# A decoder layer on one core: branch b's values projected 512 columns wide, gates and a merge projection as filler, q's factor moved into the sigmoid

## The chip, the cores and the metric

The kernel runs on one core of a Trainium2 chip. The time is that of the device, in microseconds, from the first to the last instruction with what little lies around it. The engines are TensorE (PE), VectorE (DVE), ScalarE (ACT), GpSimd (POOL) and SyncE (SP), which issues nearly all DMAs. Each works through its own list of instructions in order, and waits at an instruction until what it needs is there.

## The reference, cut to what matters

One layer for 512 tokens of width 1024, in float32:

```python
h = rms_norm(x, g_mix)
qa, ka, va, qb, kb, vb, gates = jnp.split(h @ w_in, IN_SPLITS, axis=-1)
ya = moba_attention(rope(qa), rope(ka), va)             # 8 heads of 64, causal softmax
yb = stick_breaking_attention(qb, kb, vb)               # 8 heads of 64
#   z = q k^T / 8;  a = sigmoid(z) * (product of 1 - sigmoid(z) over the later keys)
g = sigmoid(gates + b_gate)                             # 2 x 1024
x = x + (g[0] * (ya @ w_branch_a) + g[1] * (yb @ w_branch_b)) @ w_out
u_gate, u_val = split(causal_depthwise_conv(rms_norm(x, g_ffn) @ w_up))
x = x + (silu(u_gate) * u_val) @ w_down                 # 2816 wide
return rms_norm(x, g_final)
```

With 512 tokens and blocks of 256, branch a's attention (moba) is a causal softmax over all keys.

## The kernel before

**Products.** Every large float32 product is made of three matmuls of rounded parts: both operands are split into a high part (`hi`, an ACT copy to a shorter format) and the rest (`lo`, a DVE subtraction), and hi.hi, hi.lo and lo.hi are added up in PSUM (`mm3`, called a triple here). `wload` fetches 512 KB of weights by DMA into `raw`, ACT makes `whi` (L67), DVE makes `wlo` (L68); there are three buffers of each, so a split waits until TensorE is through with the weights three loads back.

**Order.** TensorE's instructions run in the order in which the code is written (`manual_schedule`); those of DVE, ACT, POOL and SP are ordered by a scheduler when the kernel is built.

**The stages.** First `qk0`, the projection of branch a's first q and k from `xg` (8 tiles of x times g_mix, split, not yet normalised), while DVE adds up the squares `ssq`; a product of `ssq` with ones gives the row sums, `rstd_cols` and `rsqrt` (L114 to L131) turn them into r1, a 128x4 tile, and `bcast_rows` transposes r1 into `rb`, a tile with r along the columns. It scales everything that was projected from `xg`. Then `vproj_a` projects branch a's values, 512 columns a matmul. Then the attention: `attend(branch, pairs, gaps)` works on four heads (two pairs) at a time, twice for each branch. Its steps are `score` for a unit of query tiles (unit 0 has tiles 0 and 1, unit 1 tile 2, unit 2 tile 3), the weights on DVE, ACT and (branch b) POOL, and `turn`, the transposes of the weights of a unit and pair into the PSUM tile `tp`, of which there is one; ACT (branch b, and odd units of a) or DVE copies it to `aT`. Branch a's weights are maxima (L327), exponentials with their sums, and a multiply (L337); branch b's are two sigmoids, selects for the diagonal on POOL, scans (L357) and a multiply (L359). After the last step the attention products `av` follow, and ACT and DVE split their result into `ya` or `yb`.

**Filler.** Between two steps `fill(gap)` puts so many triples of other work into TensorE's list: the rest of branch a's q and k (`moba_qk`, whose results are rotated on DVE), branch b's q and k (`sb_qk`), branch b's values (`vproj_b`, 256 columns a matmul, half a unit each), and the first gates. Each such projection accumulates into one of two PSUM banks (`mm`), so the next but one can't start before DVE or ACT have taken its result out. What is left of the fillers runs after the last attention product (`fill(1000)`). The merge then makes, for each of 8 column tiles, the projections of `ya` and of `yb`, each multiplied by its gate. Behind it come W_out, the feed-forward part and the final norm, which the change leaves alone.

## Time and profile before

| | |
|---|---|
| median of 3 runs | 746.32 us (746.0 to 746.59) |
| the profiled execution | 746.52 us, of which 744.8 us are the span from first to last instruction |
| granted TensorE clock, mean | 0.998 |
| busy, share of the span | PE 99%, DVE 60%, ACT 41%, POOL 3% |
| matmuls on PE | 3890 |

The profile shows one execution: its page gives busy shares, waits and the chain of work that ended last, and its trace can be asked for a timeline of any stretch. In the rows a matmul's `us` is its length, and lengths overlap: what counts for the time is the distance from start to start. `x4` behind a row means four instructions in one row. Buffer numbers are left out.

### The profile page before, as it was taken

Reading aid. Unit: us, or ns where it says so; the run is one execution under the profiler, and the core shown is the slowest. Engines: PE = TensorE matmul, PEld = TensorE weight load, DVE = VectorE, ACT = ScalarE, POOL = GpSimd, SP = SyncE. Lnnn points to the kernel's source line nnn. Section 1 sums busy time; section 2 is a strip of 40 time slices with the busy share of each in tenths; the row PEclk is TensorE's granted clock in tenths of the full one; section 3 lists DMA queues with packets and bytes.
Section 4 is the critical chain, followed back from the end, with each engine's and each line's share of the span. In section 5 each row is a group of like instructions: output and inputs, shape, how many; then the busy total and the mean of one; then the engine's idle time right before and its main releaser. Section 6 shows DMA issues by size and latency. Waiting matters only on the chain.

```text
span 744.8 us, 9628 instructions
## 1 busy us (share of the span) xinstructions
PE 734.5 (99%) x3890; PEld 610.5 (82%) x3890; DVE 449.2 (60%) x635; ACT 306.5 (41%) x437; POOL 21.7 (3%) x40
## 2 busy tenths in 40 slices
PE   9999999999999999999999999999999999999996
PEld 6788888879788888888888888888888888888885
DVE  6868876692964544545658767777676774121233
ACT  6345453563652332324335444443544442121233
POOL 0000000320310000000000000000000000000000
PEclk9999999999999999999999999999999999999999
DMA  8332211121225323223232232323223232323203
GB/s 311 118 96 75 75 41 57 41 78 53 87 85 173 111 84 114 85 94 105 90 108 86 90 108 85 114 85 103 95 89 110 85 113 88 111 86 113 85 29 113
DMA packets 22364, 72.03 MB, mean 97 GB/s; under 512 B 2480, under 2 KB 3120, under 8 KB 22320
## 3 DMA queue, kind: packets, MB, share of 16 engines
q1 hardware_dynamic: 21600, 70.24, 28.4%
q10 hardware_dynamic: 720, 1.18, 0.4%
q8 instruction: 30, 0.49, 0.3%
q14 instruction: 14, 0.11, 0.1%
HBM read 69.31 MB, written 2.10 MB: 96 GB/s over the span
## 4 chain that ended last, share of the span: by engine, by line
PE 79%; issue 19%; DVE 1%; ACT 0%; POOL 0%; POOLq 0%; DVEq 0%; ACTq 0%
PE mm L72 20%; PE mm L74 20%; PE mm L73 20%; PE d L74 5%; PE d L73 5%; PE d L72 5%; PE tp L404 1%; PE tp L386 1%; PE sc L319 1%; DVE R L357 1%; PE d L553 0%; DVE a L359 0%; DVE wlo L68 0%; PE tp L117 0%; DVE on L592 0%
## 5 line engine op out<-in xcount | busy, mean ns | idle before, releaser
L67 ACT ACTIVATE whi<-raw 128x1024 fp32r<-128x1024 f32 (+2 forms) x128 | 130.1, 1021 | 225.5 <-PE mm L73 76.3
L68 DVE TENSOR_TENSOR wlo<-raw,whi 128x1024 fp32r<-128x1024 f32 (+2 forms) x128 | 149.6, 1174 | 88.8 <-ACT whi L67 87.7
L72 PE MATMUL mm<-h,whi 128*128 128x512 f32 x352 | 137.1, 390 | 0.0
L74 PE MATMUL mm<-h,wlo 128*128 128x512 f32 x352 | 137.0, 389 | 0.0
L73 PE MATMUL mm<-h,whi 128*128 128x512 f32 x352 | 136.9, 389 | 0.0
L72 PE MATMUL mm<-xg,whi 128*128 128x512 f32 x224 | 89.9, 401 | 0.0
L74 PE MATMUL mm<-xg,wlo 128*128 128x512 f32 x224 | 87.4, 390 | 0.0
L73 PE MATMUL mm<-xg,whi 128*128 128x512 f32 x224 | 87.3, 390 | 0.0
L73 PEld LDWEIGHTS mm<-h,whi 128*128 128x128 f32 x352 | 66.1, 188 | 13.8
L72 PEld LDWEIGHTS mm<-h,whi 128*128 128x128 f32 x352 | 66.1, 188 | 13.7
L74 PEld LDWEIGHTS mm<-h,wlo 128*128 128x128 f32 x352 | 66.1, 188 | 13.6
L72 PE MATMUL d<-whi,gT 128*128 128x512 f32 x176 | 69.2, 393 | 0.0
L73 PE MATMUL d<-wlo,gT 128*128 128x512 f32 x176 | 68.5, 389 | 0.0
L74 PE MATMUL d<-whi,gT 128*128 128x512 f32 x176 | 68.5, 389 | 0.0
L526 DVE TENSOR_TENSOR u<-mm,rb 128x512 f32<-128x512 f32 x44 | 30.2, 688 | 38.3 <-PE mm L74 38.3
L72 PEld LDWEIGHTS mm<-xg,whi 128*128 128x128 f32 x224 | 42.1, 188 | 9.7 <-issue 1.4
L74 PEld LDWEIGHTS mm<-xg,wlo 128*128 128x128 f32 x224 | 42.1, 188 | 9.1
L73 PEld LDWEIGHTS mm<-xg,whi 128*128 128x128 f32 x224 | 42.2, 188 | 7.8
L74 PEld LDWEIGHTS d<-whi,gT 128*128 128x128 f32 x176 | 33.0, 188 | 6.8
L73 PEld LDWEIGHTS d<-wlo,gT 128*128 128x128 f32 x176 | 33.1, 188 | 6.6
L72 PEld LDWEIGHTS d<-whi,gT 128*128 128x128 f32 x176 | 33.1, 188 | 6.6
L251 ACT ACTIVATE gT<-t 128x512 fp32r<-128x512 f32 x22 | 13.9, 632 | 58.7 <-DVE t L535 58.6
(160 smaller groups left out, 1034.1 us busy)
## 6 DMA issues: line engine op xcount, KB each, us to landing
raw<-w SPq DMA_DIRECT2D x118, 512.0 KB, 3.3
xk<-xT SPq DMA_DIRECT2D x8, 256.5 KB, 5.6
x1T<-xT SPq DMA_DIRECT2D x8, 256.0 KB, 5.2
raw<-w SPq DMA_DIRECT2D x6, 256.0 KB, 6.0
out<-on ACTq DMA_DIRECT2D x4, 256.0 KB, 2.8
out<-on SPq DMA_DIRECT2D x4, 256.0 KB, 2.7
tg<-trig SPq DMA_DIRECT2D x1, 512.0 KB, 6.6
gb<-gfin SPq DMA_DIRECT2D x1, 512.0 KB, 3.7
```

The costliest lines, as they stand in the source:

```text
L67: nc.scalar.activation(hi[:, sl], raw[:, sl], AF.Copy)
L68: nc.vector.tensor_sub(lo[:, sl], raw[:, sl], hi[:, sl].bitcast(F32))
L72: nc.tensor.matmul(ps, a[0], b[0], start=start, stop=False)
L73: nc.tensor.matmul(ps, a[0], b[1], start=False, stop=False)
L74: nc.tensor.matmul(ps, a[1], b[0], start=False, stop=stop)
L251: nc.scalar.activation(hl[:, 0], o, AF.Copy)
L319: nc.tensor.matmul(sc[:, h, o:o + n], q[r0:r0 + 64, c, qt * 128:(qt + 1) * 128], k[r0:r0 + 64, d, :n], start=m == 0, stop=m == 2, skip_gro ...
L357: nc.vector.tensor_tensor_scan(R[:, h, r0:r0 + n][:, ::-1], z[:, ::-1], z, 1.0, op0=OP.mult, op1=OP.bypass)
L386: nc.tensor.transpose(tp[:, h, c:c + 128], a[:, h, c:c + 128], ident)
L404: nc.tensor.matmul(av[h * 64:(h + 1) * 64, j, qt * 128:(qt + 1) * 128], v[:, kb, (2 * p + h) * 64:(2 * p + h + 1) * 64], aT[p][:, h, o + k ...
L526: nc.vector.tensor_mul(u, ps, rb2)
```

## The change

- Branch b's values are projected by the same function as branch a's (`vproj`), right behind them, 512 columns a matmul, in the PSUM banks of `qk0`.
- Four column tiles of gates instead of three are filler, and with each of them branch a's projection of the merge and its multiply (`branch(i, 0, ...)`), with half-size weight loads. The merge loop keeps branch b's half for these four.
- Branch b's q is no longer scaled by r and 1/8. It is split straight from PSUM, and the sigmoids take the factor as a scale for each query row (`rq`, plus and minus r1/8), one sigmoid for each query tile. So a DVE instruction of 512 columns (L283) goes for each pair, and unit 0 has four sigmoids a pair instead of two.
- The product of ones and `ssq` stands four matmuls later, behind two of the last tile's three groups of four.
- 8 triples of filler stand ahead of the attention; in branch a score 2 comes one turn later, and one list of gaps is changed. The fillers are 176 triples before and after.
- The warm-up tile is set in another pool, and a padding tile is 88 wide instead of 72.

```diff
--- before.py
+++ after.py
@@ -23,10 +23,10 @@
 FF = 2816
 FT = FF // 128
 EPS = 1e-6
-NG = 3
+NG = 4
 NWARM = 9 * (448,) + (128,)
 LAST = 4
...
@@ -52,18 +52,19 @@
     consts = pool(ctx, "consts", 1)
     wraw = pool(ctx, "wraw", 3)
     wsp = pool(ctx, "wsp", 3)
-    def wload(key, pieces=1, dst=None, eng=None):
+    def wload(key, pieces=1, dst=None, eng=None, half=None):
         raw = wraw.tile([128, 1024], F32, name="raw")
         hi = (dst or wsp).tile([128, 1024], F32R, name="whi")
         lo = (dst or wsp).tile([128, 1024], F32R, name="wlo")
         n = 1024 // pieces
-        for i in range(pieces):
-            sl = slice(i * n, (i + 1) * n)
+        sls = [slice(i * n, (i + 1) * n) for i in range(pieces)]
+        if half is not None:
+            sls = [slice(half * 512, (half + 1) * 512)]
+        for i, sl in enumerate(sls):
             (eng if eng is not None and i == 0 else nc.sync).dma_start(raw[:, sl], w[WIDX[key]][:, sl])
...
-        for i in range(pieces):
-            sl = slice(i * n, (i + 1) * n)
+        for sl in sls:
             nc.scalar.activation(hi[:, sl], raw[:, sl], AF.Copy)
             nc.vector.tensor_sub(lo[:, sl], raw[:, sl], hi[:, sl].bitcast(F32))
         return hi, lo
@@ -83,8 +84,6 @@
...
-    warmb = consts.tile([128, 448], BF, name="warmb")
-    nc.vector.memset(warmb, 0.0)
     ident = consts.tile([128, 128], F32, name="ident")
     make_identity(nc, ident)
...
-    padt = pad.tile([128, 72], F32, name="padt")
+    padt = pad.tile([128, 88], F32, name="padt")
     nc.vector.memset(padt, 0.0)
...
@@ -144,6 +143,8 @@
     p1 = pool(st1, "p1", 1, PSUM)
     ssq = xp.tile([128, S], F32, name="ssq", bufs=1)
     qk0 = [p1.tile([128, S], F32, name=f"q{j}") for j in range(4)]
+    warmb = xp.tile([128, 448], BF, name="warmb", bufs=1)
+    nc.vector.memset(warmb, 0.0)
     warm = pmm.tile([128, 512], F32, name="mm")
     for n in NWARM:
         nc.tensor.matmul(warm[:, :n], warmb[:, :128], warmb[:, :n], start=True, stop=True)
@@ -181,29 +182,32 @@
             for j in range(k - 2, KT):
                 square(j)
         for n, (i, j) in enumerate(((0, 0), (0, 1), (1, 0))):
-            if k == KT - 1 and n == 1:
+            if k == KT - 1 and n == 2:
                 r1 = rstd_cols(ssq, pmm, "mm", "n1")
             for c in range(4):
                 nc.tensor.matmul(qk0[c], w0[i][:, (k % 2) * 512 + c * 128:(k % 2) * 512 + (c + 1) * 128],
                                  xg[k][:, j], start=(k == 0 and n == 0), stop=(k == KT - 1 and n == 2))
     bcast_rows(r1, pmm, "mm", rb)
-
-    def vproj_a():
-        ps = [pool_.tile([128, S], F32, name=n) for pool_, n in ((p1, "v0"), (p1, "v1"), (pmm, "mm"), (pmm, "mm"))]
+    rq = [consts.tile([128, QT], F32, name=f"rq{i}") for i in range(2)]
+    for i, c in enumerate((-0.125, 0.125)):
+        nc.vector.tensor_scalar(rq[i], r1, c, None, op0=OP.mult)
+
+    def vproj(name, dst, banks):
+        ps = [pool_.tile([128, S], F32, name=n) for pool_, n in banks]
         for k in range(KT):
             if k % 2 == 0:
-                wt = wload(("va", k // 2))
+                wt = wload((name, k // 2))
             for t in range(QT):
                 a = (xg[k][:, 0, t * 128:(t + 1) * 128], xg[k][:, 1, t * 128:(t + 1) * 128])
                 mm3(ps[t], a, blk(wt, k % 2, 512), k == 0, k == KT - 1)
         for t in range(QT):
             if t % 2:
-                nc.scalar.activation(va[:, t], ps[t], AF.Copy, scale=r1[:, t:t + 1])
+                nc.scalar.activation(dst[:, t], ps[t], AF.Copy, scale=r1[:, t:t + 1])
             else:
-                nc.vector.tensor_scalar(va[:, t], ps[t], r1[:, t:t + 1], None, op0=OP.mult)
+                nc.vector.tensor_scalar(dst[:, t], ps[t], r1[:, t:t + 1], None, op0=OP.mult)
 
     mqkp = pool(ysta, "mqkp", 4, side="right")
-    hlp = pool(ysta, "hlp", 2, side="right")
+    hlp = pool(ysta, "hlp", 1, side="right")
     mst = ExitStack()
     mp = pool(mst, "mp", 1, side="right")
     va = mp.tile([128, QT, 512], F32, name="va")
@@ -222,23 +226,6 @@
                 yield 1.0
         use(ps)
         yield 1.0
-
-    def vproj_b(g):
...
@@ -278,10 +265,9 @@
         sc = {}
 
         def use(n, nm, ps):
-            o = hlp.tile([128, S], F32, name="o")
-            if nm == "q":
-                nc.vector.scalar_tensor_tensor(o, ps, 0.125, rb, op0=OP.mult, op1=OP.mult)
-            else:
+            o = ps
+            if nm == "k":
+                o = hlp.tile([128, S], F32, name="o")
                 nc.vector.tensor_mul(o, ps, rb)
             sc[nm] = mqkp.tile([128, 2, S], F32R, name=f"hl{n}")
             split_out(sc[nm], o)
@@ -340,9 +326,10 @@
     def weights_b(sc, seg):
         W = seg[-1][1] + seg[-1][2]
         s1 = att.tile([128, 2, 512], F32, name="a1")
-        nc.scalar.activation(s1[:, :, :W], sc[:, :, :W], AF.Sigmoid, scale=-1.0)
         be = att.tile([128, 2, 512], F32, name="a2")
-        nc.scalar.activation(be[:, :, :W], sc[:, :, :W], AF.Sigmoid)
+        for i, z in enumerate((s1, be)):
+            for qt, o, n in seg:
+                nc.scalar.activation(z[:, :, o:o + n], sc[:, :, o:o + n], AF.Sigmoid, scale=rq[i][:, qt:qt + 1])
         for z, fill in ((s1, 1.0), (be, 0.0)):
             for qt, o, n in seg:
                 zz = z[:, :, o + n - 128:o + n]
@@ -390,8 +377,8 @@
             else:
                 nc.vector.tensor_copy(aT[p][:, :, o:o + W], tp[:, :, :W])
 
-        steps = [(score, 0), (score, 1)] + [(turn, 0, p) for p in pairs] + [(score, 2)]
-        steps += [(turn, u, p) for u in (1, 2) for p in pairs]
+        steps = [(score, 0), (score, 1)] + [(turn, u, p) for u in range(3) for p in pairs]
+        steps.insert(5 if br == "a" else 4, (score, 2))
         for (f, *args), gap in zip(steps, gaps):
             f(*args)
             fill(gap)
@@ -414,12 +401,24 @@
         half = {}
         for i in range(2):
             rotate(0, n, i, qk0[2 * n + i], half)
-    vproj_a()
+    vproj("va", va, ((p1, "v0"), (p1, "v1"), (pmm, "mm"), (pmm, "mm")))
+    vproj("vb", vb, [(p1, f"q{j}") for j in range(4)])
     st1.close()
     atp = pool(asta, "atp", 2)
     att = pool(asta, "att", 2)
     psc = pool(psA, "psc", 2, PSUM)
     ptr = pool(psA, "ptr", 1, PSUM)
+    def branch(i, b, g):
+        wt = wload(("ab", i), half=b)
+        ps = pmm.tile([128, S], F32, name="mm")
+        for p in range(4):
+            y = yhl["ab"[b], p]
+            mm3(ps, blk(wt, b * 4 + p), (y[:, 0], y[:, 1]), p == 0, p == 3)
+            if p < 3:
+                yield 1.0
+        nc.vector.tensor_mul(g, g, ps)
+        yield 1.0
+
     def gates(i):
         pend[i] = []
 
@@ -429,14 +428,15 @@
             nc.scalar.activation(g, g, AF.Sigmoid, bias=bgate[:, b * 8 + i:b * 8 + i + 1])
             pend[i].append(g)
 
-        for b in range(2):
-            yield from proj(("g", i, b), lambda ps: use(b, ps))
+        yield from proj(("g", i, 0), lambda ps: use(0, ps))
+        yield from branch(i, 0, pend[i][0])
+        yield from proj(("g", i, 1), lambda ps: use(1, ps))
 
     pend = {}
-    fillers = [moba_qk(1), sb_qk(0), sb_qk(1), vproj_b(0), sb_qk(2), sb_qk(3), vproj_b(1)]
-    fillers += [gates(i) for i in range(NG)]
+    fillers = [moba_qk(1)] + [sb_qk(p) for p in range(4)] + [gates(i) for i in range(NG)]
+    fill(8)
     GAPS_A = (12, 0, 5, 5, 0, 5, 7, 5, 5)
-    GAPS_A2 = (10, 0, 3, 6, 0, 3, 6, 3, 3)
+    GAPS_A2 = (10, 0, 3, 6, 0, 5, 4, 3, 3)
     GAPS_B = (8, 4, 5, 4, 3, 5, 7, 5, 5)
     attend("a", (0, 1), GAPS_A)
     attend("a", (2, 3), GAPS_A2)
@@ -444,7 +444,7 @@
     ybp = pool(ysta, "ybp", 1, side="right")
     for p in range(4):
         yhl["b", p] = ybp.tile([128, 2, S], F32R, name=f"yb{p}")
-    gsig = pool(ysta, "gsig", 6, side="right")
+    gsig = pool(ysta, "gsig", 2 * NG, side="right")
     attend("b", (0, 1), GAPS_B)
     attend("b", (2, 3), GAPS_B)
     fill(1000)
@@ -461,22 +461,18 @@
     x1T = [x1p.tile([128, S], F32, name=f"x1T{k}") for k in range(KT)]
     for k in range(KT):
         nc.sync.dma_start(x1T[k], xT[k][:, :S])
-    mtp = pool(mst, "mtp", 2)
 
     for i in range(KT):
         if i >= NG:
             fillers.append(gates(i))
             fill(1000)
-        wab = wload(("ab", i))
         g = pend[i]
-        for b, br in enumerate("ab"):
-            ps = pmm.tile([128, S], F32, name="mm")
-            for p in range(4):
-                mm3(ps, blk(wab, b * 4 + p), (yhl[br, p][:, 0], yhl[br, p][:, 1]), p == 0, p == 3)
-            nc.vector.tensor_mul(g[b], g[b], ps)
+        for _ in branch(i, 1, g[1]):
+            pass
         nc.vector.tensor_add(g[0], g[0], g[1])
         split_out(mhl[i], g[0])
     ysta.close()
+    mtp = pool(mst, "mtp", 2)
     hst = ExitStack()
     x1s = pool(hst, "x1s", 1, side="right")
     h2 = [x1s.tile([128, 2, S], F32R, name=f"h2{k}") for k in range(KT)]
...
```

The scheduled orders, at three places. Here is DVE's list around r1: `ssq` is the sum of squares, `n1v`, `n1t` and `n1r` are steps to r1, `wlo` are weight splits. Before:

```order
L158 TENSOR_TENSOR ssq<-ssq,sq 128x512 [waits DVE_49,Activation_49] x2
L119 TENSOR_SCALAR n1v<-mm 128x4 [waits PE_49]
L126 RECIPROCAL n1r<-n1s 128x4 [waits Activation_49]
L128 TENSOR_TENSOR n1t<-n1r 128x4 [waits DVE_49]
L129 SCALAR_TENSOR_TENSOR n1t<-n1t,n1v 128x4 [waits DVE_49]
L130 SCALAR_TENSOR_TENSOR n1r<-n1t,n1r 128x4 [waits DVE_49]
L68 TENSOR_TENSOR wlo<-raw,whi 128x1024 [waits DMAHW6_49,PE_49,Activation_49]
L137 COPY rb<-mm 128x512 [waits PE_49]
```

After the change:

```order
L159 TENSOR_TENSOR ssq<-ssq,sq 128x512 [waits DVE_49,Activation_49] x3
L69 TENSOR_TENSOR wlo<-raw,whi 128x1024 [waits DMAHW5_49,PE_49,Activation_49]
L159 TENSOR_TENSOR ssq<-ssq,sq 128x512 [waits DVE_49,Activation_49]
L118 TENSOR_SCALAR n1v<-mm 128x4 [waits PE_49]
L125 RECIPROCAL n1r<-n1s 128x4 [waits Activation_49]
L127 TENSOR_TENSOR n1t<-n1r 128x4 [waits DVE_49]
L69 TENSOR_TENSOR wlo<-raw,whi 128x1024 [waits DMAHW6_49,PE_49]
L128 SCALAR_TENSOR_TENSOR n1t<-n1t,n1v 128x4 [waits DVE_49]
L129 SCALAR_TENSOR_TENSOR n1r<-n1t,n1r 128x4 [waits DVE_49]
L193 TENSOR_SCALAR rq_355<-n1r 128x4 [waits DVE_49]
```

The split that stood behind the last step (third weight of branch a's values) stands between the third and the fourth step of r1, and the split of the second weight has moved ahead of the last addition to `ssq`.

DVE's list in branch a, pairs 0 and 1, from the weights of unit 0 (`a`) to the first copy of `aT`; `r` are the rotated projections, `hl` their split parts. Before:

```order
L337 TENSOR_SCALAR a_620<-a_620,st 128x256 x2
L260 SCALAR_TENSOR_TENSOR r_663<-mm,tg 128x512
L260 SCALAR_TENSOR_TENSOR r_664<-mm,tg 128x512
L68 TENSOR_TENSOR wlo<-raw,whi 128x1024
L327 TENSOR_REDUCE st<-sc 128x2 x2
L391 COPY aT<-tp 128x2x384
L333 RECIPROCAL st<-st 128x2
```

After the change:

```order
L323 TENSOR_SCALAR a_787<-a_787,st 128x256 x2
L247 SCALAR_TENSOR_TENSOR r_830<-mm,tg 128x512
L247 SCALAR_TENSOR_TENSOR r_831<-mm,tg 128x512
L252 TENSOR_TENSOR r_710<-r_710,r_830 128x512
L69 TENSOR_TENSOR wlo<-raw,whi 128x1024
L252 TENSOR_TENSOR r_709<-r_709,r_831 128x512
L239 TENSOR_TENSOR hl_839<-r_710,hl_839 128x512
L239 TENSOR_TENSOR hl_835<-r_709,hl_835 128x512
L313 TENSOR_REDUCE st<-sc 128x2 x2
L378 COPY aT<-tp 128x2x384
L319 RECIPROCAL st<-st 128x2
```

Two additions (L252) and two splits (L239) have come to stand ahead of unit 1's maxima (TENSOR_REDUCE) and of the copy of `aT`.

DVE's list in branch b, pairs 0 and 1, from the second pair's scans of unit 0 (`R`) to those of unit 1; `hl<-mm` is the split of the unscaled q, `o<-mm` a scaled projection. Before:

```order
L357 SCALAR_TENSOR_TENSOR R<-a_1557 128x128 x2
L357 SCALAR_TENSOR_TENSOR R<-a_1557 128x256 x2
L240 TENSOR_SCALAR vb<-mm,n1r 128x256
L354 MEMSET R 128x2
L359 TENSOR_TENSOR a_1559<-a_1559,R 128x2x128
L68 TENSOR_TENSOR wlo<-raw,whi 128x1024
L359 TENSOR_TENSOR a_1559<-a_1559,R 128x2x256
L354 MEMSET R 128x2
L357 SCALAR_TENSOR_TENSOR R<-a_1631 128x384 x2
L283 SCALAR_TENSOR_TENSOR o<-mm,rb 128x512
L357 SCALAR_TENSOR_TENSOR R<-a_1644 128x384 x2
L68 TENSOR_TENSOR wlo<-raw,whi 128x1024
```

After the change:

```order
L344 SCALAR_TENSOR_TENSOR R<-a_1682 128x128 x2
L341 MEMSET R 128x2
L344 SCALAR_TENSOR_TENSOR R<-a_1682 128x256 x2
L346 TENSOR_TENSOR a_1683<-a_1683,R 128x2x128
L69 TENSOR_TENSOR wlo<-raw,whi 128x512
L346 TENSOR_TENSOR a_1683<-a_1683,R 128x2x256
L239 TENSOR_TENSOR hl_1711<-mm,hl_1711 128x512
L341 MEMSET R 128x2
L344 SCALAR_TENSOR_TENSOR R<-a_1753 128x384 x2
L271 TENSOR_TENSOR o<-mm,rb 128x512
L344 SCALAR_TENSOR_TENSOR R<-a_1766 128x384 x2
```

An eviction of branch b's values (L240) and a 1024-wide weight split are gone, a 512-wide one stands in its place; the split of q (L239) stands behind the multiplies of unit 0, where before the scaling of q (L283) emptied its bank behind two scans of unit 1.

## Rows read from the trace of the kernel before

**Rows 1.** The page: busy time of each engine, and the chain that ended last.
```profile
PE 734.5 (99%) x3890; PEld 610.5 (82%) x3890; DVE 449.2 (60%) x635; ACT 306.5 (41%) x437; POOL 21.7 (3%) x40
...
PE 79%; issue 19%; DVE 1%; ACT 0%; POOL 0%; POOLq 0%; DVEq 0%; ACTq 0%
```

**Rows 2.** Waits of TensorE, whole span: total us, times, longest us.
```profile
PE tp L386 <- ACT aT L389: 1.7, 2, 1.0
...
PE mm L117 <- DVE ssq L158: 0.7, 1, 0.7
```

**Rows 3.** Timeline of PE, 24 to 29 us: start, us, engine line, operands, [idle before].
```profile
24.04 1.07 PE L187 MATMUL q<-xg,whi 128*128 128x512 f32 x4
25.80 1.05 PE L117 MATMUL mm<-ones,ssq 128*128 128x2 f32 x8 [0.69 <-DVE ssq L158]
...
28.65 0.60 PE L136 MATMUL mm<-ident,n1r 128*128 128x128 f32 x4
```

**Rows 4.** Timeline of DVE, same stretch.
```profile
24.26 1.48 DVE L158 TENSOR_TENSOR ssq<-ssq,sq 128x512 f32<-128x512 f32 x2
...
27.53 0.16 DVE L128 TENSOR_TENSOR n1t<-n1r 128x4 f32<-128x4 f32 x1
...
27.93 0.16 DVE L130 SCALAR_TENSOR_TENSOR n1r<-n1t,n1r 128x4 f32<-128x4 f32 x1
29.01 1.23 DVE L68 TENSOR_TENSOR wlo<-raw,whi 128x1024 fp32r<-128x1024 f32 x1 [0.92 <-ACT whi L67]
```

**Rows 5.** Timeline of PE, 117 to 119 us, and a PE group by shape.
```profile
117.31 0.39 PE L74 MATMUL mm<-xg,wlo 128*128 128x512 f32 x1
117.54 0.28 PE L72 MATMUL mm<-whi,xg 128*128 128x256 f32 x1
...
118.86 0.28 PE L74 MATMUL mm<-whi,xg 128*128 128x256 f32 x1
...
L72 PE MATMUL mm<-whi,xg 128*128 128x256 f32 x64 | 18.7, 292 | 0.0
```

**Rows 6.** Timelines of PE and DVE, 50 to 68 us.
```profile
50.90 0.62 PE L301 MATMUL sc<-maskb,identb 128*128 128x128 bf16 x8
...
60.80 1.28 DVE L260 SCALAR_TENSOR_TENSOR r<-mm,tg 128x512 f32<-128x512 f32 x2
...
64.86 0.94 DVE L391 COPY aT<-tp 128x768 f32<-128x768 f32 x1
...
67.08 0.82 PE L386 MATMUL tp<-ident,a 128*128 128x128 f32 x6
```

**Rows 7.** Timelines of ACT and PE, 118 to 120 us.
```profile
118.92 0.81 ACT L389 ACTIVATE aT<-tp 128x768 f32<-128x768 f32 x1
...
119.79 0.88 PE L386 MATMUL tp<-ident,a 128*128 128x128 f32 x6 [0.64 <-ACT aT L389]
```

**Rows 8.** Timelines of PE and DVE, 135 to 153 us.
```profile
135.46 1.64 PE L319 MATMUL sc<-hl,hl 64*128 64x128 f32 x24
...
145.05 0.45 DVE L240 TENSOR_SCALAR vb<-mm,n1r 128x256 f32<-128x256 f32 x1
...
146.91 0.89 DVE L359 TENSOR_TENSOR a<-a,R 128x512 f32<-128x512 f32 x1
...
152.34 0.87 PE L386 MATMUL tp<-ident,a 128*128 128x128 f32 x6 [1.03 <-ACT aT L389]
```

**Rows 9.** Timelines of PE and DVE, 182 to 200 us.
```profile
182.80 1.64 PE L319 MATMUL sc<-hl,hl 64*128 64x128 f32 x24
...
193.51 0.67 DVE L359 TENSOR_TENSOR a<-a,R 128x512 f32<-128x512 f32 x1
...
198.84 0.66 DVE L428 TENSOR_TENSOR g<-mm,rb 128x512 f32<-128x512 f32 x1
```

**Rows 10.** Timelines of PE and DVE, 228 to 232 us.
```profile
228.43 0.50 PE L72 MATMUL mm<-xg,whi 128*128 128x512 f32 x1
...
230.54 0.69 DVE L411 TENSOR_TENSOR yb<-tp,yb 128x512 fp32r<-128x512 f32 x1 [0.66 <-ACT yb L410]
```

More of the change, by code (lines that the diff above doesn't have):

```diff
@@ L25 @@
 EPS = 1e-6
-NG = 3
+NG = 4
 NWARM = 9 * (448,) + (128,)
 LAST = 4
-WORDER = ([(n, k) for n in ("qk0", "va") for k in range(4)] + [("vb", g, h) for g in range(2) for h in range(2)]
+WORDER = ([(n, k) for n in ("qk0", "va", "vb") for k in range(4)]
           + [("mqk", n, i) for n in range(2) for i in range(2)] + [("sqk", p, n) for p in range(4) for n in range(2)]
@@ L611, in pack @@
             t["mqk", n, i] = rows(w_in, halves(base, 1, i))
-    for j in range(4):
-        t["va", j] = rows(w_in[j * 256:(j + 1) * 256], 1024 + np.arange(512))
-    for g in range(2):
-        for h in range(2):
-            t["vb", g, h] = rows(w_in[h * 512:(h + 1) * 512], 2560 + g * 256 + np.arange(256))
+    for n, base in (("va", 1024), ("vb", 2560)):
+        for j in range(4):
+            t[n, j] = rows(w_in[j * 256:(j + 1) * 256], base + np.arange(512))
     for p in range(4):
```

15 lines of the change are left out of this document (removed).

## The prediction

> **What bounds the kernel now.** I read the page first, then TensorE's waits, then the timelines of the stretches that the change touches. TensorE is busy for 734.5 us of the 744.8 us span, and the chain of work that ended last is TensorE's matmuls at 79% with 19% of issue between them [rows 1]. A time therefore changes only where TensorE gets fewer or cheaper instructions, or waits more or less. The list of its waits is short [rows 2]: 1.7 us in two waits on ACT's copy of transposed attention weights (`aT`), 0.7 us on `ssq`, the sum of squares, and the first weight and memset of the start. (The list counts from the end of the matmul before; below I count from when the next start was due.) DVE, ACT and POOL cost something only where TensorE stands behind one of their instructions, and all four run their own lists in order. So I took the changed lists of DVE and ACT, laid the durations of the old rows along them, and compared each release with the time at which TensorE arrives. An arrival is a start plus matmuls at 0.227 us, plus 0.1 us for the first one after transposes or scores; a DVE release reaches TensorE about 0.06 us after its end (`ssq` ends at 25.74, the matmul starts at 25.80 [rows 3, 4]).
>
> The sum is made against the profiled execution, 746.52 us, which is 0.2 us above the median of 746.32.
>
> **Term 1, branch b's values 512 wide: -1.2 us.** A matmul of 512 columns starts 0.23 us after its predecessor; twelve of 256 columns start from 117.54 to 118.86, 0.120 us apart, and three lines have 64 of these each [rows 5]. So 192 x 0.120 = 23.0 us are removed, and 96 of 512 columns at 0.2266 us (the mean of many starts; a single row shows 0.22 or 0.23) are put in, 21.8 us: -1.2 to -1.3, and I take -1.2. Bounds: -1.0 (a spacing of 0.1185, the middle of the 64 of each line) to -1.3.
> On this edit the Trainium skill (TensorE: Matmul & The Clock Gate, Back-to-back issue gap) gives the isolated gap at full clock as columns/2.4 + 2.5 ns. That would be 109.2 and 215.8 ns, a saving of only 0.25 us, and a sum 0.95 us higher than mine. Both widths are 11 ns further apart in the rows, which makes the narrow ones dearer; the rows decide.
>
> **Term 2, the row scale r1 and its broadcast: +1.0 us.** Before, TensorE stands 0.85 us until `ssq` is done (the four starts from 24.04 on would have gone on at 24.95; 25.80 came), then has eight matmuls that cover the small chain on DVE, and the broadcast's transposes start at 28.65 directly behind them [rows 3]. After, the `ssq` product stands four matmuls later. That hides most of the 0.85: those four end at 25.86, and `ssq`, whose last addition now stands behind a weight split, ends near 25.90, so 0.1 of wait is left. But only four matmuls (26.87 to 28.04) then stand in front of the transposes. And in DVE's new list a weight split of 1024 columns has slipped in between the second and the third step of the chain. It overwrites a buffer that those four matmuls read, so it can't start before 28.08; it runs 1.23 us as its like does, and the two steps behind it (0.2 each from start to start) end at 29.6 [rows 4]. The transposes start at 29.65 instead of 28.65, after a wait of 1.6 to 1.8 us with the whole engine queue behind it. ACT also has a split's first half ahead of the square root now, but it waits only for matmuls that end before the product starts, and is done (27.0) when the square root's input is. Bounds: +0.8 (no wait on `ssq`, and the steps overlapping the split's tail) to +1.2.
>
> **Term 3, branch a, pairs 0 and 1: +0.9 us.** The front block of 8 triples moves the rotation of the second group's queries earlier against the scores. So DVE has two additions and two low-half splits (0.6 us each: two instructions of 512 columns take 1.28 there, and the next begins 0.08 before the second ends [rows 6]) ahead of unit 1's maxima and of the copy of the first `aT`. Before, that copy ended 14.9 us after score 0 began (50.90 to 65.80), and the next turn's transposes, which need its PSUM tile, came 16.2 us after it (67.08) [rows 6]: slack 1.3. After, the copy ends 2.4 us later by these four instructions, less about 0.3 since the split ahead of the first maxima no longer queues behind the eviction of the values: 17.0, against an arrival at 16.2. Bounds +0.5 to +1.2.
>
> **Term 4, branch a, pairs 2 and 3: -0.8 us.** ACT's copy of the odd unit stands behind the exponentials of unit 2, ends at 119.73, and the transposes come at 119.79, 0.8 late [rows 7]. With score 2 moved behind the first turn of unit 1 that copy goes ahead of those exponentials, 4 us before it is asked for. Nothing else there is nearer than 0.4 us. Bounds -0.85 to -0.3.
>
> **Term 5, branch b, pairs 0 and 1: +0.6 us.** Before, the last transposes before score 2 wait at 152.34 behind ACT's copy: 1.25 us [rows 8]. That wait goes. But the unscaled q is now split straight out of PSUM, and this split (DVE) is what frees the bank; it stands behind the scans and multiplies of unit 0. DVE turns from those scans to its next work at 145.05, 9.6 us after score 0 began at 135.46 [rows 8]; then follow a multiply of 0.4, a 512-wide weight split of 0.6, a multiply of 0.65 and the split itself, 0.7 (estimates; instructions of 512 columns take 0.64 to 0.67 in [rows 6, 9]); less 0.35, as a sigmoid of one query tile lets POOL and the first scan begin sooner. That is 11.6. TensorE asks for the bank after 1.58 of scores, 8 triples, 1.25 of scores and 6 matmuls: 9.8. A wait of 1.8 in place of 1.25. If the bank came in time, the old wait would return at about 0.95; so bounds -0.3 to +1.0.
>
> **Term 6, branch b, pairs 2 and 3: +0.7 us.** Nothing waits there before. Score 0 begins at 182.80, and the gate's multiply behind unit 1's four scans ends at 199.50, 16.7 later [rows 9]. The new list drops an eviction (0.4) and a 1024-wide split (1.13), adds a multiply (0.6) and begins 0.35 sooner: 15.4. Its bank is now asked for at 14.65 (scores 1.58, eight triples 5.54, scores 1.25, 12 matmuls, a turn, 12 matmuls). Bounds 0 to +1.2.
>
> **Term 7, into the merge: +0.5 us.** Six triples of gates stood behind the last attention product, and covered the splits of branch b's outputs. With branch a's projections done as filler, none is left (8 in front and 168 units against gaps of 170). The last low half ends at 231.23, 2.80 after the start of TensorE's first matmul behind the product (228.43) [rows 10]; with the release 2.86. The tenth matmul, which needs it, now comes at 2.38. Bounds +0.2 to +0.8.
>
> **At nothing:** the later warm-up memset (0.1 us; the warm-up matmuls run into a wait for the first weight anyway), the half-size weight loads (each issued over 5 us before its use), the saved q multiplies on DVE, the split sigmoids on ACT (part of terms 5 and 6). [...]
>
> Sum: -1.2 + 1.0 + 0.9 - 0.8 + 0.6 + 0.7 + 0.5 = **+1.7**, so 748.2 for a profiled run and 748.0 at the median. The bounds add up to -0.9 to +4.3.
>
> **Rivals.** A change below 0.2%, 1.49 us, can't be told from none here: 744.8 to 747.8 counts as the same.
> *The broadcast isn't held (same).* If the inserted split is done early or doesn't wait for those four matmuls, the chain ends as it did (28.09 [rows 4]) plus the 0.16 by which `ssq` is later, the transposes start at 28.3 instead of 29.65, and term 2 is -0.3: 746.7. For it: DVE has nothing else to do while TensorE runs the four. Against: the split writes a buffer that they read. It decides the verdict once the wait there is under about 1.4 us.
> *The lists keep up in attention (same).* Terms 3, 5 and 6 at their low ends, +0.5 - 0.3 + 0 instead of 2.2: 746.0. For it: each wait makes TensorE later, so slack grows downstream. Against: the new instructions stand in lists that were without a gap at these places.
> *All waits go (faster).* If the old waits (0.85, 0.8, 1.25 and 0.1 of small ones) go and no new one appears: -1.2 - 3.0, 742.1. Term 7 and the split in term 2 speak against it.
> *Scans and multiplies slow (slower).* A pair of multiplies of 256-wide rows took 0.89 us beside POOL's selects [rows 8] and 0.67 elsewhere [rows 9]. If POOL's earlier start costs DVE 0.2 on four instructions in each of terms 5 and 6, that is +1.6: 749.6. For it: POOL's selects begin sooner and lie beside more of DVE's work; against: there are no more of them.
> *The spacing rule.* If 256-wide matmuls cost what columns alone make of them, term 1 is -0.25: 749.0. The rows already speak against it.
> *The change doesn't do what it says.* It would not if the gates' work still stood behind the last attention product; its order shows that it doesn't, and I give it no chance of its own.
>
> **How the numbers follow.** Forecast 0.50; broadcast not held 0.12; lists keep up 0.15; all waits go 0.08; slowed scans 0.12; spacing 0.03. The forecast's own spread is 746.7 to 749.4, and about a quarter of it (0.12) lies under 747.8. Slower: 0.38 + 0.12 + 0.03 = 0.53; faster: 0.08 and the far end of the second rival, 0.11; same: the rest, 0.36. The range leaves out the fast rival and the far end of the slow one: 745.2 to 749.7.
>
> **What would show it.** Term 1: no matmuls of 256 columns in projections, 0.227 us between all. Term 2: TensorE's wait before the transposes on DVE's r1, 1.6 to 1.8 us, and 0.1 on `ssq`. Term 3: a wait of the second pair's turn on DVE's `aT` copy near 0.9. Term 4: no wait on ACT there. Terms 5 and 6: waits for a matmul bank on a DVE split of q (1.8) and on a gate's multiply (0.7). Term 7: 0.5 on branch b's last split. I am wrong if DVE's chain for r1 ends before 28.3, or if the waits on DVE in attention add up to under 2 us.

## The result, and the profile after

The changed kernel takes 750.99 us (750.36 to 751.14, 6 runs) against 746.26 us (6 runs) before: the ratio is 1.0062, with a 95% interval of 1.0049 to 1.0075. It is slower, as forecast, but by 4.7 us and not by 1.7, and above the end of the range. The profiled execution took 751.14 us, with a span of 749.2.

The page of the changed kernel, as [rows 1] of the kernel before: busy time, and the chain that ended last.

```profile
PE 736.5 (98%) x3794; PEld 607.0 (81%) x3794; DVE 447.2 (60%) x639; ACT 311.3 (42%) x451; POOL 21.8 (3%) x40
...
PE 88%; issue 6%; DVE 4%; ACT 1%; POOL 0%; DVEq 0%; POOLq 0%; ACTq 0%
```

TensorE issues 96 matmuls fewer and is busy for 2.0 us longer. TensorE's waits after the change (total us, times, longest us; L135 are the broadcast's transposes, L373 those of the attention weights, L73 and L74 matmuls of projections):

```profile
PE mm L135 <- DVE n1r L129: 1.7, 1, 1.7
PE mm L73 <- DVE hl L239: 1.5, 1, 1.5
...
PE mm L73 <- DVE g L427: 0.8, 1, 0.8
PE tp L373 <- DVE aT L378: 0.7, 1, 0.7
PE mm L74 <- DVE yb L398: 0.2, 1, 0.2
```

Both waits of [rows 2] are gone, and five on DVE stand in their place. First the front, where the largest was forecast. PE's timeline from 26.7 us on:

```profile
26.70 0.95 PE L116 MATMUL mm<-ones,ssq 128*128 128x2 f32 x8
27.51 1.19 PE L188 MATMUL q<-xg,wlo 128*128 128x512 f32 x4
30.38 0.83 PE L135 MATMUL mm<-ident,n1r 128*128 128x128 f32 x4 [1.68 <-DVE n1r L129]
30.87 0.78 PE L73 MATMUL v<-whi,xg 128*128 128x512 f32 x1
31.44 0.63 PE L74 MATMUL v<-wlo,xg 128*128 128x512 f32 x1
31.87 0.63 PE L75 MATMUL v<-whi,xg 128*128 128x512 f32 x1
...
34.27 0.39 PE L75 MATMUL mm<-whi,xg 128*128 128x512 f32 x1
```

The product of ones starts at 26.70, the four matmuls behind it at 27.51, the transposes at 30.38 after a wait of 1.68 us. DVE in the same stretch shows why:

```profile
28.34 0.16 DVE L127 TENSOR_TENSOR n1t<-n1r 128x4 f32<-128x4 f32 x1
28.74 1.23 DVE L69 TENSOR_TENSOR wlo<-raw,whi 128x1024 fp32r<-128x1024 f32 x1 [0.24 <-PE q L188]
29.88 0.16 DVE L128 SCALAR_TENSOR_TENSOR n1t<-n1t,n1v 128x4 f32<-128x4 f32 x1
30.07 0.16 DVE L129 SCALAR_TENSOR_TENSOR n1r<-n1t,n1r 128x4 f32<-128x4 f32 x1
```

The weight split starts at 28.74, when the last of the four matmuls is done, and the two steps of r1 behind it end at 30.23. That is the forecast's picture, 0.7 us later. What it lacked is in PE's rows from 30.87 on: the next matmuls start 0.57 and 0.43 us apart, where they were 0.23 apart in [rows 5]. Windows of the same execution, each 1 us (PE, PEld, DVE, ACT, POOL busy with counts, then the granted clock as a share of 2.4 GHz, and the DMA):

```profile
29.00:30.00 1.00, 0.00 (x0) 0.00 (x0) 1.00 (x2) 0.00 (x0) 0.00 (x0) 1.00 0.00 0
30.00:31.00 1.00, 0.62 (x5) 0.65 (x5) 0.44 (x4) 0.00 (x0) 0.00 (x0) 0.82 0.00 0
31.00:32.00 1.00, 1.00 (x5) 0.81 (x4) 0.71 (x2) 0.00 (x0) 0.00 (x0) 0.50 0.67 225
...
33.00:34.00 1.00, 1.00 (x3) 0.71 (x3) 1.00 (x3) 0.00 (x0) 0.00 (x0) 0.50 0.00 0
34.00:35.00 1.00, 1.00 (x6) 0.81 (x5) 1.00 (x3) 0.00 (x0) 0.00 (x0) 0.97 0.00 0
```

Behind the wait the granted clock is 0.50, 1.2 GHz, until 34. From the first matmul of the values to the start of the ninth, 3.40 us pass (30.87 to 34.27); in the same run of nine in experiment 4 below (30.74 to 32.66) it is 1.92. So 1.48 us went to the clock, and another 0.12 in the transposes ahead of them: 0.49 us from their start to the first matmul, for 0.37 in experiment 4.

And the 0.7 us by which all this is late come from the very start. PE's first rows after the change, and the row of the kernel before that answers to the second:

```profile
1.35 3.65 PE L150 MATMUL mm<-warmb 128*128 128x448 bf16 x10 [1.35 <-DVE R L341]
4.78 3.03 PE L188 MATMUL q<-xg,whi 128*128 128x512 f32 x8
```

```profile
4.87 2.11 PE L187 MATMUL q<-xg,whi 128*128 128x512 f32 x8 [0.24 <-ACT whi L67]
```

The first eight matmuls of the first projection cover 3.03 us and not 2.11; by their starts (4.78, 5.37, 5.79, 6.22, 6.65) they are 0.43 us apart from the second to the fifth, the spacing that goes with 0.50 in the rows above. The column of the granted clock reads 1.00 in this stretch, but it has nothing to read there: the trace's list of clock levels begins with the full level at 6.75 us here, and at 4.25 us in the kernel before.

Cut into stretches by the same landmarks, the two traces differ so (after less before; triples that were only moved are taken out at 0.68 us each; a stretch of the attention goes from the start of one score 0 to the next, branch b's last one to the attention products):

| stretch | forecast | measured | worked out from |
|---|---|---|---|
| 192 narrow matmuls to 96 wide | -1.2 | -1.3 | 23.0 before; 54.26 to 75.80 plus one spacing, 21.77 |
| start up to the first values | +1.0 | +1.87 | 29.00 to 30.87; 0.12 of it is the clock's |
| clock behind the wait | 0 | +1.48 | above |
| branch a, pairs 0, 1 | +0.9 | +1.0 | length 44.96 to 45.96 |
| branch a, pairs 2, 3 | -0.8 | -0.7 | 39.60 to 38.37, with 0.56 of narrow matmuls taken out |
| branch b, pairs 0, 1 | +0.6 | +0.45 | 47.34 to 47.24, plus 0.56 |
| branch b, pairs 2, 3 | +0.7 | +1.0 | 41.12 to 40.62, plus 1.36 of two triples, plus 0.16 |
| into the merge | +0.5 | +0.55 | rest of the span; 0.44 of it at one matmul, 261.02 for 260.58 |

The sum is 4.4, the difference of the spans (744.8 to 749.2); it has to be, as the last row is what is left. These are the projection of branch b's values, the first and the last matmul:

```profile
54.26 0.39 PE L73 MATMUL q<-whi,xg 128*128 128x512 f32 x1
...
75.80 0.39 PE L75 MATMUL q<-whi,xg 128*128 128x512 f32 x1
```

The waits in the attention, each with the DVE instruction that ends it: the copy of `aT` in branch a, and the split of the unscaled q in branch b.

```profile
97.54 0.95 DVE L378 COPY aT<-tp 128x768 f32<-128x768 f32 x1
...
98.55 0.66 PE L373 MATMUL tp<-ident,a 128*128 128x128 f32 x4 [0.72 <-DVE aT L378]
```

```profile
176.74 0.68 DVE L239 TENSOR_TENSOR hl<-mm,hl 128x512 fp32r<-128x512 f32 x1
...
177.47 0.50 PE L73 MATMUL mm<-xg,whi 128*128 128x512 f32 x1 [1.52 <-DVE hl L239]
```

The copy ends at 98.49 and the transposes start at 98.55; the split ends at 177.42 and the matmul starts at 177.47, 1.91 us after the one before it. The latter is the longest of the attention's waits, 1.7 us beyond the usual spacing, and the matmuls behind it are 0.23 apart: the clock held there.

### The profile page after: what moved, and what is told of

Read it like the earlier page. It is cut to its first block, busy times and chain, and to the rows that moved or that the text cites. A ratio compares the mean times of both kernels' runs of the same rounds, so it can differ in the third digit from the quotient of the medians.

```text
span 749.2 us, 9486 instructions
## 1 busy us (share of the span) xinstructions
PE 736.5 (98%) x3794; PEld 607.0 (81%) x3794; DVE 447.2 (60%) x639; ACT 311.3 (42%) x451; POOL 21.8 (3%) x40
## 4 chain that ended last, share of the span: by engine, by line
PE 88%; issue 6%; DVE 4%; ACT 1%; POOL 0%; DVEq 0%; POOLq 0%; ACTq 0%
PE mm L73 20%; PE mm L74 20%; PE mm L75 20%; PE d L75 5%; PE d L74 5%; PE d L73 5%; PE q L188 3%; PE tp L373 2%; DVE R L344 1%; PE tp L391 1%; PE sc L295 1%; PE q L74 1%; PE q L73 1%; PE q L75 1%; DVE wlo L69 1%
## 5 line engine op out<-in xcount | busy, mean ns | idle before, releaser
L68 ACT ACTIVATE whi<-raw 128x1024 fp32r<-128x1024 f32 (+2 forms) x136 | 131.7, 972 | 218.5 <-PE mm L74 89.8
L73 PE MATMUL mm<-h,whi 128*128 128x512 f32 x352 | 137.1, 390 | 0.0
L74 PE MATMUL mm<-h,whi 128*128 128x512 f32 x352 | 136.9, 389 | 0.0
L73 PE MATMUL mm<-xg,whi 128*128 128x512 f32 x224 | 90.2, 403 | 2.3 <-DVE hl L239 1.5
L74 PE MATMUL mm<-xg,whi 128*128 128x512 f32 x224 | 87.4, 390 | 0.0
L74 PEld LDWEIGHTS mm<-h,whi 128*128 128x128 f32 x352 | 66.1, 188 | 13.8
L73 PEld LDWEIGHTS mm<-h,whi 128*128 128x128 f32 x352 | 66.1, 188 | 13.6
L73 PE MATMUL d<-whi,gT 128*128 128x512 f32 x176 | 69.2, 393 | 0.0
L74 PE MATMUL d<-wlo,gT 128*128 128x512 f32 x176 | 68.5, 389 | 0.0
L73 PEld LDWEIGHTS mm<-xg,whi 128*128 128x128 f32 x224 | 42.1, 188 | 13.1 <-issue 2.8
L74 PEld LDWEIGHTS mm<-xg,whi 128*128 128x128 f32 x224 | 42.2, 188 | 7.8
L74 PEld LDWEIGHTS d<-wlo,gT 128*128 128x128 f32 x176 | 33.1, 188 | 6.6
L73 PEld LDWEIGHTS d<-whi,gT 128*128 128x128 f32 x176 | 33.1, 188 | 6.6
```

The costliest lines, as they stand in the source:

```text
L68: nc.scalar.activation(hi[:, sl], raw[:, sl], AF.Copy)
L73: nc.tensor.matmul(ps, a[0], b[0], start=start, stop=False)
L74: nc.tensor.matmul(ps, a[0], b[1], start=False, stop=False)
```

## The experiments

All are compared with the kernel before on the same chip, 746.2 to 746.3 us throughout. "The front" is the stretch up to the projection of the values.

**1. Warm-up first.** The memset of the warm-up tile goes ahead of the two others on DVE, as before the change.

```diff
-    nc.vector.memset(ones, 1.0)
...
-    nc.vector.memset(padt, 0.0)
...
     nc.vector.memset(warmb, 0.0)
+    nc.vector.memset(ones, 1.0)
+    nc.vector.memset(padt, 0.0)
```

> The changed kernel with the memset of the warm-up tile first on DVE again, as before the change. Theory (the warm-up began 0.13 us later, and for that the first five matmuls of the first projection ran at 0.427 us spacing, the lower clock level): the five are at 0.227 again, 0.9 to 1.0 us less than the changed kernel, 750.0 us; nothing else moves. Rival (the slow start comes from something else in the changed kernel, the 0.13 us are hidden): 751.0 us, and the five stay at 0.427.

Measured: 750.46 us (748.66 to 751.94, 5 runs). The profiled execution starts its warm-up at 1.22 us as the kernel before, and is slow all the same:

```profile
1.22 3.65 PE L150 MATMUL mm<-warmb 128*128 128x448 bf16 x10 [1.22 <-DVE warmb L145]
5.06 2.94 PE L188 MATMUL q<-xg,whi 128*128 128x512 f32 x8 [0.19 <-ACT whi L68]
```

Eight matmuls in 2.94 us. The theory on the start is refuted by this row; the 0.13 us are not what makes it slow. Its executions spread by 3.3 us, so its median says little: this one has a span of 749.4 us at a mean clock of 0.996, two others 746.8 and 746.9 at 0.999.

**2. The split behind r1.**

```diff
+            if (name, k) == ("va", 4):
+                with tc.issue_after(rlast.ins):
+                    wt = wload((name, 2))
-            if k % 2 == 0:
+            elif k % 2 == 0:
```

> The changed kernel with the third weight split of branch a's values held behind the last step of r1 on DVE. Theory (wait of 1.85 us before the broadcast's transposes, and seven matmuls at the lower clock level behind it): transposes 1.3 us earlier, no matmul at 0.427 us near 31 us, 1.35 + 1.45 = 2.8 us less than the changed kernel, 748.2 us. Rival (the lower level there doesn't hang on the wait): only 1.35 us less, 749.6 us, and seven matmuls at 0.427 us still.

Measured: 748.07 us (747.34 to 748.69, 10 runs), 2.9 less than the changed kernel. The wait on r1, and PE's rows at the start and behind the transposes:

```profile
PE mm L138 <- DVE n1r L132: 0.3, 1, 0.3
...
4.98 2.11 PE L191 MATMUL q<-xg,whi 128*128 128x512 f32 x8
...
25.98 0.95 PE L116 MATMUL mm<-ones,ssq 128*128 128x2 f32 x8
...
28.32 0.62 PE L138 MATMUL mm<-ident,n1r 128*128 128x128 f32 x4 [0.35 <-DVE n1r L132]
...
29.00 0.39 PE L74 MATMUL v<-wlo,xg 128*128 128x512 f32 x1
29.23 0.40 PE L75 MATMUL v<-whi,xg 128*128 128x512 f32 x1
```

The wait is 0.3 us, the matmuls behind it are 0.23 apart, and the theory's sum is met within 0.2 us. But the profiled execution also began fast (2.11 us, with the late memset). Against the changed kernel's trace the product of ones comes 0.72 us earlier (25.98 for 26.70), which is the start's; the transposes come another 1.34 earlier, and the ninth matmul behind them another 1.59 (30.62 for 34.27). The last two are the theory's 2.8. The spans of the ten lie at 745.5 to 745.7 (four) and at 746.2 to 746.4 (six); the six are as far below the changed kernel's 749.2 as the last two make, which fits a slow start in both, but no trace of the six is kept.

**3. Both edits.**

> Both edits, warm-up first and split held back. Theory: the two add up, 747.2 us, still about 0.9 us over the kernel before, by the waits in the attention (0.9, 1.7 for 1.25, 1.0) and into the merge (0.45) less what the change gains. Rival (the two losses of clock are one and the same, the late start is what makes the later one): with the start mended the second gains nothing more than its wait, 748.6 us.

Measured: 747.71 us (747.17 to 748.86, 10 runs), 0.4 less than the second alone. That is 0.5 above the theory's figure and 0.9 below the rival's; the warm-up's place adds nothing that these spreads show.

**4. TensorE kept busy in the wait.**

```diff
+    keep = p1.tile([128, S], F32, name="v0")
+    for _ in range(9):
+        nc.tensor.matmul(keep[:, :448], warmb[:, :128], warmb, start=True, stop=True)
     bcast_rows(r1, pmm, "mm", rb)
```

> The changed kernel, with nine extra matmuls of 448 bf16 columns (zeros, into a PSUM bank that is written later) in the wait before the broadcast's transposes; the wait itself stays as long, since DVE is late all the same. Theory (TensorE standing still is what brings the lower level): no matmul at 0.427 us near 31 us, 1.45 us less than the changed kernel, 749.6 us (up to 0.2 more if the nine outlast the wait). Rival (something else in that stretch brings it): 751.0 us or more.

Measured: 749.19 us (748.69 to 749.61, 4 runs), 1.8 less than the changed kernel, with nothing else done than to fill the wait:

```profile
26.69 0.95 PE L116 MATMUL mm<-ones,ssq 128*128 128x2 f32 x8
...
28.53 1.88 PE L192 MATMUL v<-warmb 128*128 128x448 bf16 x9
30.37 0.62 PE L135 MATMUL mm<-ident,n1r 128*128 128x128 f32 x4
30.74 0.48 PE L73 MATMUL v<-whi,xg 128*128 128x512 f32 x1
31.06 0.40 PE L74 MATMUL v<-wlo,xg 128*128 128x512 f32 x1
...
32.66 0.39 PE L75 MATMUL mm<-whi,xg 128*128 128x512 f32 x1
```

This execution began fast (2.11 us for the first eight matmuls), but a wait of 0.55 us on ACT at 8.38 took that back: the product of ones comes at 26.69, for 26.70 in the changed kernel's trace. The transposes come at 30.37, as late as there (30.38), and from the second matmul behind them on the spacing is 0.23. By the ninth this trace is 1.61 us ahead, and its span is 1.6 us shorter (747.6 for 749.2). So the lower level there hangs on TensorE standing still, and it is worth 1.6 us.

**5. The kernel before with the product moved, nothing else.**

```diff
-            if k == KT - 1 and n == 1:
+            if k == KT - 1 and n == 2:
```

> The kernel before, with the product of ones and the sum of squares four matmuls later and nothing else; the schedule then puts the weight split between the steps of r1 as in the changed kernel. Theory (this one edit makes both the wait and the lower clock level behind it): a wait of 1.7 us before the transposes in place of 0.85 on the sum of squares, about seven matmuls at 0.427 us behind it, +1.0 +1.45, 748.7 us. Rival (the lower level comes only with other parts of the change): +1.0, 747.3 us, all matmuls behind the wait at 0.227.

Measured: a median of 749.53 us, but in two groups: four executions at 747.33 to 747.87 and six at 749.50 to 749.88, with nothing between. The profiled one is of the lower group. Its wait, and the window behind it:

```profile
PE mm L136 <- DVE n1r L130: 1.7, 1, 1.7
...
30.00:31.00 1.00, 1.00 (x7) 0.82 (x6) 0.74 (x2) 0.00 (x0) 0.00 (x0) 1.00 0.73 221
```

The same wait of 1.7 us, and the granted clock stays 1.00. The lower group is at +1.1 to +1.6, the rival's figure, and the trace shows the clock holding. The upper group is at +3.2 to +3.6, 0.8 to 1.2 above the theory's 748.7. No trace of it is kept. Its mean granted clock is 0.995 in five of the six, against 0.997 to 0.999 in the lower group, and a fall as long as the changed kernel's lowers the mean by 0.002; the 0.8 to 1.2 are near the 0.7 to 1.0 that a slow start cost in the traces of the changed kernel and of experiment 6. That both came together in that group is likely but not shown. Nor is a wait of this length needed for a long execution: one of the thirty of the kernel before beside this run took 748.91 us, at 0.996. What is shown is that the wait doesn't force the fall of the clock. In the changed kernel all six executions had a mean of 0.996 or 0.997.

**6. The kernel before with the late warm-up.**

```diff
-    nc.vector.memset(warmb, 0.0)
...
-    padt = pad.tile([128, 72], F32, name="padt")
+    padt = pad.tile([128, 104], F32, name="padt")
...
+    warmb = xp.tile([128, 448], BF, name="warmb", bufs=1)
+    nc.vector.memset(warmb, 0.0)
```

> The kernel before, with the warm-up tile's memset behind the two other memsets on DVE and nothing else. Theory, as the first four runs left it (the memset's 0.13 us don't set when the clock rises at the start, it varies from execution to execution): 746.3 to 746.5 us, or a spread of executions of up to 1 us. Rival (a later warm-up shifts the rise to 6.7 us in every execution): 747.3 us, five matmuls at 0.427 us near 5 us.

Measured: 746.42 us (746.13 to 747.03, 10 runs), the ratio 0.9999 (0.999 to 1.0009): no change. The profiled execution is the longest of the ten, and it shows what became of a slow start in the kernel before (PE's rows, then DVE's last addition to `ssq`):

```profile
1.37 3.65 PE L149 MATMUL mm<-warmb 128*128 128x448 bf16 x10 [1.37 <-DVE R L354]
4.84 3.13 PE L187 MATMUL q<-xg,whi 128*128 128x512 f32 x8
...
26.27 1.05 PE L115 MATMUL mm<-ones,ssq 128*128 128x2 f32 x8
```

```profile
25.53 0.69 DVE L158 TENSOR_TENSOR ssq<-ssq,sq 128x512 f32<-128x512 f32 x1
```

Eight matmuls take 3.13 us, 1.0 us more than in the kernel before, yet the product of ones starts at 26.27, 0.47 later than in [rows 3]. It starts 0.05 us after `ssq` is done (26.22), so the wait still stands there, but it has shrunk: the product was due at 25.97, four spacings behind 25.06, and waits 0.30 us from then on where it waited 0.85 before. So about half of the slow start was taken up by the wait that the change removes. In the changed kernel nothing is taken up: against experiment 2's trace it is 0.71 us late behind the first eight matmuls (7.64 for 6.93) and 0.72 at the product.

**7. Score 2 of branch a one turn later, nothing else**, with the change's list of gaps.

> The kernel before, with branch a's score 2 one turn later and the list of gaps of its second half as in the change, nothing else. Theory: TensorE's wait of 0.8 us at 119.8 on ACT's copy goes and nothing takes its place, 745.5 us. Rival (the copies of the next turns are late instead): 746.3 us, with waits of 0.5 us or more between 118 and 133 us.

Measured: 745.68 us (745.18 to 746.18, 10 runs), the ratio 0.999 (0.998 to 1.0). The wait at 119.8 is gone and nothing took its place. It is 0.6 us, by the theory's side, at the edge of what can be told from no change.

**8. q scaled on DVE again**, on top of the second.

```diff
-            o = ps
-            if nm == "k":
-                o = hlp.tile([128, S], F32, name="o")
+            o = hlp.tile([128, S], F32, name="o")
+            if nm == "q":
+                nc.vector.scalar_tensor_tensor(o, ps, 0.125, rb, op0=OP.mult, op1=OP.mult)
+            else:
                 nc.vector.tensor_mul(o, ps, rb)
...
-                nc.scalar.activation(z[:, :, o:o + n], sc[:, :, o:o + n], AF.Sigmoid, scale=rq[i][:, qt:qt + 1])
+            nc.scalar.activation(z[:, :, :W], sc[:, :, :W], AF.Sigmoid, scale=c)
```

> The changed kernel with the split held behind r1 (as the second run), and branch b's q scaled on DVE again with one sigmoid for unit 0, as before the change. Theory (the split of the unscaled q, behind unit 0's multiplies, is what frees the bank late): the 1.5 us wait on that split goes, and a wait of 1.0 to 1.3 us on the copy of the transposed weights stands in its place, as before; 747.6 us against 748.07. Rival (DVE is simply too full there, whichever instruction frees the bank): the wait stays within 0.2 us of 1.5 on the scaling, and the instruction more on DVE makes the other bank wait longer, 748.1 to 748.8 us.

Measured: 748.0 us (747.3 to 749.57, 9 runs), no change against the second. TensorE's two longest waits in branch b:

```profile
PE tp L379 <- ACT aT L382: 1.3, 1, 1.3
PE mm L73 <- DVE g L433: 1.3, 1, 1.3
```

The wait on the split of q is gone, and one of 1.3 us on ACT's copy stands in its place, as forecast; the second wait, on the gate's multiply, grew from 0.8 to 1.3 us, as the rival has it for a fuller DVE. The two cancel: moving q's factor into the sigmoid is worth nothing here, in either direction.

**9. No triples in front**, on top of the second: `fill(0)` for `fill(8)`.

> The changed kernel with the split held behind r1, and no triples in front of the attention instead of 8 (what is left over, 6 triples, then stands behind the last attention product). Theory (the 8 in front are what puts the rotation ahead of unit 1's maxima, and what takes the cover from branch b's last split): the waits of 0.9 near 97 us and of 0.45 near 260 us go, 746.7 us against 748.07. Rival (the first only moves to another copy, since DVE has as much to do): 747.6 us, only the last wait gone.

Measured: 744.82 us (744.22 to 745.97, 10 runs), the ratio to the kernel before 0.9982 (0.9973 to 0.9991), 1.9 us less than the theory's figure. TensorE's waits:

```profile
PE sc L293 <- ACT vb L211: 0.5, 1, 0.5
PE mm L73 <- DVE hl L245: 0.5, 1, 0.5
```

Not only the two waits of the theory went: the split of q now ends 0.5 us late, not 1.5, and the gate's multiply isn't waited for at all, while the copy of branch b's values is waited for at the first scores, 0.5 us, where the 8 triples stood between before.

**10. Four triples in front**, on top of the second: `fill(4)`.

> The same with 4 triples in front (2 left behind the last attention product). Theory: the wait of 0.45 into the merge goes, and the one near 97 us stays if the rotation's four instructions still stand ahead of unit 1's maxima on DVE: 747.6 us; if they don't, 746.7. Rival: branch b's two waits for a bank (1.5 and 0.8 to 1.0 us) change with the shift by more than that, since a projection then ends at another point of the scans: outside 746.3 to 748.3 us.

Measured: 748.51 us (746.35 to 749.0, 6 runs), above either figure of the theory. The median lies outside the rival's range, by 0.2 us, and three of the six executions inside it. Branch b's two waits are gone, which is the rival's mechanism, but what makes the time is another thing. One wait in the attention is left, and it is long; behind it the clock's level:

```profile
PE tp L379 <- DVE aT L384: 2.4, 1, 2.4
...
97.00:98.00 1.00, 1.00 (x4) 0.79 (x3) 0.79 (x3) 0.00 (x0) 0.00 (x0) 0.50 0.00 0
```

2.4 us on the copy of `aT` in branch a, and the granted clock at 0.50 behind it, as in the front of the changed kernel. Five of the six executions have a mean clock of 0.995 or 0.996; the sixth has 0.998, and takes 746.35 us. So the theory's account of the first pairs isn't a matter of 8 triples or none: four make that wait longer, and the time no better than with 8 (748.07).

**11. The seventh, and two triples moved to ahead of branch b's second turn.**

```diff
+    GAPS_B1 = (8, 4, 7, 2, 3, 5, 7, 5, 5)
...
-    attend("b", (0, 1), GAPS_B)
+    attend("b", (0, 1), GAPS_B1)
```

> The kernel before with branch a's score 2 one turn later (as the seventh run), and in branch b's first half two triples moved from behind the second turn of unit 0 to ahead of it. Theory (the 1.25 us wait there comes from asking too early for ACT's copy, and two triples are 1.36 us): the wait goes, 744.5 us, 1.8 less than the kernel before. Rival (the scores that follow later make the next copies late instead): 745.7 us, with a wait of about 1 us on the next turn.

Measured: 745.84 us (745.47 to 746.01, 11 runs), as the seventh (745.68). The rival is right, and the wait's new place is the scores themselves:

```profile
PE sc L319 <- ACT a L345: 1.2, 1, 1.2
```

**12. The product back at its place, no triples in front.** From the changed kernel, `n == 1` again and `fill(0)`.

> The changed kernel with the product of ones and the sum of squares back at its place before the change, and no triples in front of the attention; the schedule then keeps the weight split behind r1 by itself. Theory (the wait on the sum of squares that the change removed took up the executions' different starts, so removing it laid them open): the transposes come at 28.7 in every execution, a wait of 0.3 to 0.9 on the sum of squares stands again, spans lie within 0.5 us of each other as with the kernel before and not within 1.1 as in the ninth run, and the median is 744.5 to 745.0 us. Rival (the starts differ by DMA or by something that both places pass on): spans spread by 1 us or more here too, median 745.2.

Measured: 744.67 us (744.14 to 746.12, 11 runs), the ratio 0.998 (0.9971 to 0.9989). A wait of 0.6 us on `ssq` stands again, the transposes come at 28.84 in the profiled execution, and the median is the theory's. Its spans run from 742.3 to 743.1, 0.8 apart, against 1.1 in the ninth and the 0.5 that was expected: narrower, but not enough to settle that the wait on `ssq` is what evens out the starts. This is the fastest version tried, 1.6 us below the kernel before; the ninth is not to be told from it.

## Why the prediction was wrong

**What failed is term 2**, the r1 chain at the front, +1.0. Its mechanism was right to the instruction: the split between the steps, its start with the end of the four matmuls, the wait of 1.6 to 1.8 us (1.68). Only the 0.1 us on `ssq` didn't come: the last addition ended at 25.49, 1.2 us ahead of the product. Two things were left out, and together they are +2.35 of the 2.7 us by which the span missed.

First, the clock. The wait was priced as time in which TensorE stands; that it comes back at 1.2 GHz was not among the rivals at all. Experiment 4 isolates it: the transposes as late as ever, TensorE busy meanwhile, the lower level gone, and 1.6 us with it. Experiment 5 shows that the wait alone doesn't bring it every time; that it needs nothing else of the change is likely from that run's upper group, but was read there from mean clocks only.

Second, the wait on `ssq` was counted as loss alone, 0.85 to be hidden. It was also slack for a slow start: experiment 6's execution lost 1.0 us at the start and half of that by the time of the product. With the product moved behind four more matmuls that cover is gone, and the changed kernel carried 0.87 more up to the first values than forecast, of which 0.12 is the clock's. That is shown for single executions; that the changed kernel's six all began slowly, and why, is not. The later memset was put at nothing, and rightly: it is refuted that its place does it (experiments 1, 2 and 6). What sets the start of an execution is left open.

**The other terms held.** Term 1 came at -1.3 for -1.2. By the Trainium skill's gap (TensorE: Matmul & The Clock Gate, Back-to-back issue gap) it would have been -0.25, an estimate from that page; the 96 matmuls at 0.227 us and the 1.3 us don't agree with that. Term 3 at +1.0, term 4 at -0.7 (alone, in experiment 7, -0.6), term 5 at +0.45, term 6 at +1.0 with the wait on the gate's multiply where it was forecast, term 7 at +0.55. None left its bounds, and outside the two stretches at the lower level the spacing was the forecast's 0.227 us. Neither of the two signs of being wrong that the prediction named came up: r1's chain ended at 30.23, and the waits on DVE in the attention add up to 3.0 us. Neither was about the clock. Two slips change nothing: the upper bounds add up to +4.1, not to +4.3, and the measured +4.4 lies above both; and the matmul that waits into the merge is the eleventh, whose due time the 2.38 is, not the tenth.

Of the rivals, the broadcast not held is refuted by the row at 28.74, and what it would be worth is borne out by experiment 2: transposes at 28.32 for the forecast 28.3. The lists didn't keep up: terms 3, 5 and 6 came to 2.45 where 2.2 was forecast. Slow scans were not needed to explain anything. That the 8 triples are to blame for terms 3 and 7 was right (experiment 9), but the waits of terms 5 and 6, put down there to the unscaled q and to the list of splits, also shrink to 0.5 us and to nothing with them: the shift of the filler against the scans decides, and which instruction frees the bank matters little (experiment 8).

## What to carry to other kernels

A wait of the engine that bounds the kernel has two prices: its length, and what the clock does behind it. A short one that stands early also takes up a part of what varies ahead of it, 0.55 of 1.0 us in experiment 6, though keeping it gained nothing that could be measured (experiment 12 against 9). When a product is moved later to hide a wait, look at what stands between it and the next use on the other engines, in the scheduled order and not in the code: here one weight split, put between two steps of 0.2 us, cost 1.3 us and the clock.
